# One layer's feed forward started by token tile: residual's bias added ahead, output units parked, first products halved

## The chip, the cores and the metric

The kernel runs on 1 core of one Trainium2 chip. Its time is the device time of one launch in microseconds (us). The engines are TensorE (PE; its weight loads are listed apart as PEld), VectorE (DVE), ScalarE (ACT), GpSimd (POOL) and SyncE (SP), whose queue issues most DMAs. Each engine works through its own list of instructions in order.

## The reference, cut to what matters

A trunk of two layers over 256 latent tokens and 256 context tokens of width 1024, in float32. Layer 1 (the second) has no context output, so its feed forward runs over the 256 latent tokens alone: two token tiles of 128.

```
m  = gated_merge of four token mixers            # out = m @ w_out + b_out
x  = layer_norm(ALPHA * x + g1 * out, ln1_g, ln1_b)
h  = layer_norm(x) * (1 + sc2) + sh2             # features of the feed forward
u  = dwconv(h @ w1 + b1)                         # 2 x 2816 columns, 3 taps over tokens
f  = (silu(gate) * val) @ w2 + b2
x  = layer_norm(ALPHA * x + g2 * f, ln2_g, ln2_b)
```

c, the conditioning vector, gives sh1 to g2 through `w_ada`: six blocks of 1024 columns per layer.

## The kernel before

Every product is taken in three parts for precision: both operands are split into a high part in float32r and a low remainder, and `mm3` (L225 to L227) issues high x high, low x high and high x low, each a 128x128 weight load and a matmul. Weights come as 1 MB blocks `raw` (two buffers, SyncE's queue, L163); `split` (L196/L194 and L198) makes `wh` on ScalarE or POOL and `wl` on VectorE or POOL, in a ring of four `wh` and four `wl`. Who casts follows a table `POOL[layer][phase]`: with (a, b, c, d), POOL takes the high part of every unit whose number leaves b when divided by a, and the remainder of every unit that leaves d when divided by c.

The layers run one after the other. In a layer, `mixer` runs four branches: recurrent, differential attention, grouped attention (`gqa`), neighbourhood attention (`na`, whose first steps are the products of n_q and n_k, evicted as `nx` at L1112). `merge` multiplies each with its branch weight and a gate into `macc`. `out_stage` then does the out projection (`acc`, eight units of w_out rows; `order` says which unit meets which token tile when) and the epilogue by token tile: `epilogue` (gate times sum, residual, layer norm with its gain and bias), `normalise` (the next layer norm, `xn`), and, once both tiles are through, `to_fm`, which transposes `xn` (`tps`, L328), applies scale and shift (`h`, L337 on VectorE and L340 on ScalarE) and splits into `hh` (POOL, L342) and `hl` (VectorE, L344).

`epilogue_prep` runs at the head of `out_stage`. It loads the gate row g and the bias row bo (L1192), doubles bo on ScalarE (L1205), multiplies both to gb on POOL (L1210), and adds gb to the residual x (L1213), the first 512 columns on VectorE, the other 512 on POOL.

Of w_out's eight units four are kept outside the ring (`wo`, made in `merge` of branch 3), the other four go through the ring. Then come the units of the feed forward: `ffn` takes them in eleven pairs, a pair being 512 columns of w1 (four units of 128 output columns, `us[0] + us[1]`), each unit 8 x 3 products over 256 tokens, evicted by ScalarE (`up`, `cv`), and the convolution's outer taps on VectorE (L1269).

`ada_step` is one quarter of a block of the w_ada product: a 1 MB load, 8 matmuls of 256 columns in column groups of 32 (16 records), and one addition (L365) on VectorE; `pump` runs steps at given places. Ahead of layer 1's first pair `pump(4)` runs the last ones, of which three have work: they belong to g2 of layer 1.

What is computed, and in which order each engine does it, is set by the order of the calls and by a scheduling layer that lays the engines' lists out. Names: `acc` is a PSUM sum of the out projection, `x_4402` and `x_4404` the two token tiles of the residual, `nmu`, `rs`, `rt`, `rstd`, `sqb`, `sqh`, `rh`, `lnb` are 128x1 statistics.

Of the kernel before, what the change touches and what calls it, by code (L numbers as in the profile page):

```python
# [8 lines left out]
F32 = mybir.dt.float32  # L9
F32R = mybir.dt.float32r  # L10
# [8 lines left out]
T = 512  # L19
# [82 lines left out]

POOL = (((4, 0, 8, 2), (4, 0, 8, 2), (4, 0, 8, 0), (5, 2, 8, 2), (6, 5, 8, 2)), ((4, 0, 4, 1), (4, 0, 4, 2), (4, 0, 100, 6), (4, 0, 4, 2), (2, 0, 4, 0)))


LATE = ((8, 8, 4, 8), (8, 8, 4, 8))
# [2 lines left out]
class Trunk:  # L111
# [32 lines left out]
    def features(self, name, w):  # L144

        out = []
        for part in "hl":
            ts = [self.Q(name + part) for _ in range(w // 128)]
            vs = [view(t, 1024 // w, w) for t in ts]
            out.append([vs[2 * j * w // 1024][:, 2 * j % (1024 // w):2 * j % (1024 // w) + 2, :] for j in range(4)])  # L150
        return out

    def S(self, name, n=1, bufs=3):
        return self.sm.tile([128, n], F32, tag=f"{name}", name=name, bufs=bufs)
# [71 lines left out]
        nc.tensor.matmul(out, lhsT=lh, rhs=rl, start=False, stop=False)  # L226
        return nc.tensor.matmul(out, lhsT=ll, rhs=rh, start=False, stop=stop)  # L227

    def fm_split(self, units, h):

        tags = [("mm", 3)] * 3 + [("o", 1)]
        ps = [self.ps.tile([128, 512], F32, tag=tags[n][0], name="mm", bufs=tags[n][1]) for n in range(len(units))]
        for a, b in ((0, SEG), (SEG, T)):
            for (hi, lo), p in zip(units, ps):
                for k in range(KD):
                    self.mm3(p[:, a:b], hi[:, k, :], lo[:, k, :], h[0][k // 2][:, k % 2, a:b],
                             h[1][k // 2][:, k % 2, a:b], k == 0, k == KD - 1)
        return ps

    def fm(self, unit, h, slices, hold=None):  # L240
        hi, lo = unit
# [325 lines left out]
    def mixer(self, l, x, hT, pool, tags):  # L567
        nc, i = self.nc, self.i
        self.pool, self.tags = pool, tags
        self.l = l  # L570
        self.with_ctx = l < DEPTH - 1
        self.hT = hT
        w = i["w_in"][l]
        self.w = w
        self.full = [(0, T)] if l == 0 else [(0, 256), (256, 512)]
        self.all = [(0, T)]
        self.lat = [(256, 512)]
        self.own = self.all if self.with_ctx else self.lat
        self.tsl = slice(0, T) if self.with_ctx else slice(SEG, T)
        self.macc = None  # L580
        if l == 1:
            us = [u for col in ("a_x", "d_k") for u in self.cols_fm(w, COL[col])]
            self.pump(PUMP[2], "s")
            ps = self.fm_split(us, hT)
            self.pre_fm = {COL["a_x"]: ps[0:2], COL["d_k"]: ps[2:4]}
        self.events, self.ready, self.phase = [], None, 0
        y = self.lru()
        gates = self.gates(0)
        self.events, self.ready, self.phase = [], None, 1
        diff = self.diff()  # L590
        next(diff)
        self.merge(0, y, gates)
        self.after_branch(1, next(diff))
        self.events, self.ready, self.phase = [], None, 2
        y = self.gqa()
        self.after_branch(2, y)
        self.events, self.ready, self.phase = [], None, 3
        y = self.na()
        self.after_branch(3, y)
# [32 lines left out]
    def merge(self, j, y, gates):  # L632
# [4 lines left out]
        if j == 3:  # L637
            box = [view(self.B("wo"), 4, D) for _ in range(2)]
            store = [None] * 2 + [lambda n=n: [(box[0][:, n, :], box[1][:, n, :])] for n in range(4)] + [None] * 2
            self.out_units = self.out_rows(self.i["w_out"][self.l], store)  # L640
            self.out_units(2), self.out_units(4)
        self.rate = rate if j < 3 else 0.0
# [554 lines left out]
    def epilogue_prep(self, l, x, segs, alloc, dep, blk, bname):  # L1197

        nc, i = self.nc, self.i
        g = {s: self.bcast(alloc, self.g_dram[l, blk][(0 if s == LAT else 1):(1 if s == LAT else 2), :], dep)  # L1200
             for s in segs}
        b = self.bcast(lambda: self.E("bo")[:, 0:512], i[bname][l:l + 1, :], dep)
        if blk == 2:
            for n in range(2):
# [2 lines left out]
        for s in segs:  # L1207
            for n in range(2):
                gb = self.E("gb")[:, 0:512]
                nc.gpsimd.tensor_tensor(out=gb, in0=g[s][n], in1=b[n], op=ALU.mult)  # L1210
                for t in x[s]:
                    xs = t[:, 512 * n:512 * n + 512]
                    eng[n].tensor_tensor(out=xs, in0=xs, in1=gb, op=ALU.add)  # L1213
        return g

    def epilogue(self, x, us, acc, g, lng, lnb, lnb_mean):

# [23 lines left out]
    def ffn(self, l, hT, nseg, apool):  # L1241
# [2 lines left out]
        W = SEG * nseg  # L1244
        w1 = i["ffn_w1"][l]
        self.a = []
        self.phase = 4
        for pair in range(NFF // 2):
            us = [list(self.cols_fm(w1, off + 256 * pair)) for off in (0, DFF)]
            if pair == 0:  # L1250
                self.pump(PUMP[0] if l == 0 else 4, "s")
            pre = self.fm_split(us[0] + us[1], hT) if pair == 0 and nseg == 2 else None
            for ci in range(2):
                jj = 2 * pair + ci
                conv = []
# [24 lines left out]
    def run(self):  # L1280
# [105 lines left out]
        self.W = SEG  # L1386
        with tc.tile_pool(name="mix1", bufs=1, reuse_waits="tile") as mp:
            self.l, self.pool = 1, mp
            self.mixer(1, None, hT, mp, {"gate": 16})
            alloc = lambda: mp.tile([128, 512], F32, tag="macc", name="epi", bufs=8)  # L1390
            x, hT2 = self.out_stage(1, {LAT: x[LAT]}, alloc, self.last_gate, (LAT,), self.m, self.out_units, KD, 8, range(2, 6), 2,
                                    "b_out", "ln1", (1, 3))
# [21 lines left out]
    def out_stage(self, l, x, alloc, dep, segs, src, units, nk, resident, kept, blk, bname, lnn, nxt):  # L1414
# [23 lines left out]
        order += [(t, k, both) for t in range(max(nt - 2, 1), nt - 1) for k in kept]  # L1438
        order += [(nt - 1, k, (n,)) for n in both for k in kept]
        self.project((srch, srcl), units, nk, order, acc)  # L1440
        hT = self.features("h", SEG * len(segs)) if nxt else None
        for s in segs:
            xn = []
            for t in range(2):
# [3 lines left out]
                if nxt:  # L1448
                    self.normalise(x[s][t], hv, nmu)
                    xn.append(hv)  # L1450
            if nxt:
                for _ in self.to_fm(*nxt, s, xn, hT[0], hT[1], SEG * segs.index(s),
                                    tags=(("t", 2), ("mm", 3) if nt == 2 else ("t", 2) if s == LAT else ("s", 2))):
                    pass
# [41 lines left out]
```

## Time and profile before

| what | value |
|---|---|
| median of 3 runs (lowest to highest) | 1539.54 us (1537.94 to 1542.12) |
| the profiled execution | 1543.09 us, of it span 1541.3 us |
| TensorE busy | 1429.6 us, 93% of the span |
| VectorE, ScalarE, POOL busy | 977.6, 638.8, 506.1 us |
| weight products `mm` (L225 to L227) of 256 and 512 columns, three parts | 507.2 + 502.2 + 502.9 us of latency, 1488 each |
| HBM read | 208.23 MB, 136 GB/s over the span |

A timeline's row gives the start in us from the span's start, the length in us, engine, line, operation, output<-input, its size and how many instructions of one kind the row holds; in square brackets stands the time for which the engine was idle before, and what released it. Lengths of matmuls overlap: the pace is read from the starts. In a row of windows, the granted clock of TensorE is a share of 2.4 GHz, 0.50 being 1.2 GHz.

### The profile page before, as it was taken

Reading aid. Unit: us, or ns where it says so; the run is one execution under the profiler, and the core shown is the slowest. Engines: PE = TensorE matmul, PEld = TensorE weight load, DVE = VectorE, ACT = ScalarE, POOL = GpSimd, SP = SyncE. Lnnn points to the kernel's source line nnn. Section 1 sums busy time; section 2 is a strip of 40 time slices with the busy share of each in tenths; the row PEclk is TensorE's granted clock in tenths of the full one; section 3 lists DMA queues with packets and bytes.
Section 4 is the critical chain, followed back from the end, with each engine's and each line's share of the span. In section 5 each row is a group of like instructions: output and inputs, shape, how many; then the busy total and the mean of one; then the engine's idle time right before and its main releaser. Section 6 shows DMA issues by size and latency. Waiting matters only on the chain.

```text
span 1541.3 us, 22344 instructions
## 1 busy us (share of the span) xinstructions
PE 1429.6 (93%) x8420; PEld 1176.3 (76%) x8420; DVE 977.6 (63%) x1691; ACT 638.8 (41%) x1136; POOL 506.1 (33%) x614
## 2 busy tenths in 40 slices
PE   5989998989999999999999999988998997899997
PEld 3757776967887777777778887887787986799876
DVE  4664655753533997554555437776875648799965
ACT  3452253233244345444444223471625353555532
POOL 2241001431432613221222412241132545366662
PEclk9999999989999999999999999998899999799999
DMA  9335612302623545444453432434432436454463
GB/s 345 118 116 184 190 69 72 127 29 67 207 81 111 179 139 167 163 138 164 160 169 124 149 133 74 145 109 141 157 129 84 146 126 208 138 165 164 165 218 109
DMA packets 149022, 218.90 MB, mean 142 GB/s; under 512 B 9990, under 2 KB 118882, under 8 KB 148914
## 3 DMA queue, kind: packets, MB, share of 16 engines
q1 hardware_dynamic: 146402, 212.74, 41.5%
q0 software_dynamic: 2512, 4.73, 1.1%
q8 instruction: 67, 1.10, 0.3%
q14 instruction: 41, 0.34, 0.1%
HBM read 208.23 MB, written 1.08 MB: 136 GB/s over the span
## 4 chain that ended last, share of the span: by engine, by line
PE 53%; DVE 12%; issue 5%; ACT 4%; DMA 4%; POOL 2%; DVEq 0%; SPq 0%; ACTq 0%; POOLq 0%
PE mm L225 12%; PE mm L226 12%; PE mm L227 11%; PE acc L227 3%; PE acc L226 3%; PE acc L225 3%; DVE wl L198 3%; DVE cv L1269 3%; PE ops L867 2%; PE adaps L362 2%; ACT wh L196 2%; PE tp L859 1%; DMA raw<-in_w_out_dram 1%; DMA raw<-in_ffn_w_dram 1%; POOL cv L1273 1%
## 5 line engine op out<-in xcount | busy, mean ns | idle before, releaser
L225 PE MATMUL mm<-hh,wh 128*128 128x256 f32 (+1 forms) x1488 | 507.2, 344 | 17.0 <-ACT gate L626 4.5
L227 PE MATMUL mm<-hh,wl 128*128 128x256 f32 (+1 forms) x1488 | 502.9, 339 | 4.5 <-DVE wl L198 3.2
L226 PE MATMUL mm<-hl,wh 128*128 128x256 f32 (+1 forms) x1488 | 502.2, 338 | 0.4 <-DVE hl L344 0.3
L198 DVE TENSOR_TENSOR wl<-raw,wh 128x1024 fp32r<-128x1024 f32 x211 | 285.8, 1362 | 176.5 <-ACT wh L196 136.8
L225 PEld LDWEIGHTS mm<-hh,wh 128*128 128x128 f32 x1488 | 287.3, 194 | 63.0 <-issue 17.2
L227 PEld LDWEIGHTS mm<-hh,wl 128*128 128x128 f32 x1488 | 287.5, 193 | 38.7 <-DVE wl L198 5.0
L196 ACT CAST wh<-raw 128x1024 fp32r<-128x1024 f32 x181 | 188.5, 1047 | 309.3 <-PE mm L226 128.1
L226 PEld LDWEIGHTS mm<-hl,wh 128*128 128x128 f32 x1488 | 287.9, 194 | 32.4 <-issue 3.6
L1269 DVE SCALAR_TENSOR_TENSOR cv<-up,par,cv 128x512 f32<-128x512 f32 (+1 forms) x176 | 156.5, 898 | 45.5 <-ACT cv L1266 33.2
L194 POOL TENSOR_SCALAR wh<-raw 128x1024 fp32r<-128x1024 f32 x74 | 89.6, 1211 | 282.9 <-PE acc L227 51.6
L198 POOL TENSOR_TENSOR wl<-raw,wh 128x1024 fp32r<-128x1024 f32 x44 | 119.0, 2704 | 129.5 <-ACT wh L196 112.0
L1273 POOL TENSOR_TENSOR cv<-cv 128x512 f32<-128x512 f32 (+1 forms) x44 | 53.5, 1216 | 158.7 <-ACT cv L1272 158.7
L226 PE MATMUL acc<-wl,a 128*128 128x512 f32 x232 | 92.3, 398 | 3.8 <-DVE wl L198 2.9
L227 PE MATMUL acc<-wh,a 128*128 128x512 f32 x232 | 92.1, 398 | 0.0
L225 PE MATMUL acc<-wh,a 128*128 128x512 f32 x232 | 91.0, 397 | 0.0
L843 DVE TENSOR_REDUCE nm<-sps 128x1 f32<-128x512 f32 (+1 forms) x96 | 56.3, 598 | 53.0 <-PE sps L888 36.9
L844 ACT ACTIVATE e<-sps,nm 128x512 f32<-128x512 f32 (+1 forms) x96 | 59.0, 617 | 64.1 <-DVE nm L843 50.3
L225 PE MATMUL mm<-wh,hh 128*128 128x256 f32 x240 | 68.6, 286 | 0.0
L227 PE MATMUL mm<-wh,hl 128*128 128x256 f32 x240 | 68.3, 284 | 0.0
L226 PE MATMUL mm<-wl,hh 128*128 128x256 f32 x240 | 67.7, 282 | 0.0
L293 ACT ACTIVATE junk<-x,nmu 128x512 bf16<-128x512 f32 x44 | 31.7, 721 | 85.0 <-DVE nmu L285 47.3
L1272 ACT ACTIVATE cv<-cv 128x512 f32<-128x512 f32 (+1 forms) x44 | 23.1, 525 | 91.4 <-DVE cv L1269 91.4
(312 smaller groups left out, 2324.5 us busy)
## 6 DMA issues: line engine op xcount, KB each, us to landing
raw<-in_ffn_w_dram SPq DMA_DIRECT2D x66, 1024.0 KB
raw<-in_w_in_dram SPq DMA_DIRECT2D x52, 1024.0 KB
raw<-in_w_ada_dram SPq DMA_DIRECT2D x40, 1024.0 KB
raw<-in_w_branch_dram SPq DMA_DIRECT2D x8, 1024.0 KB
raw<-in_w_out_dram SPq DMA_DIRECT2D x8, 1024.0 KB
w<-in_w_ada_dram SPq DMA_DIRECT2D x4, 1024.0 KB
w<-in_w_ada_dram SPq DMA_DIRECT2D x8, 512.0 KB
qk<-dp SPq DMA_DIRECT2D x48, 64.0 KB
```

The source lines that it names most:

```text
L194: nc.gpsimd.tensor_scalar(out=hi, in0=src, scalar1=1.0, scalar2=0.0, op0=ALU.mult, op1=ALU.add)
L196: nc.scalar.copy(hi, src)
L198: eng.tensor_tensor(out=lo, in0=src, in1=hi.bitcast(F32), op=ALU.subtract)
L225: nc.tensor.matmul(out, lhsT=lh, rhs=rh, start=start, stop=False)
L226: nc.tensor.matmul(out, lhsT=lh, rhs=rl, start=False, stop=False)
L227: return nc.tensor.matmul(out, lhsT=ll, rhs=rh, start=False, stop=stop)
L293: nc.scalar.activation(self.junk, halves[n], AF.Square, bias=nmu, accum_out=q[n])
L362: nc.tensor.matmul(ps[32 * g:32 * g + 32, :], lhsT=self.silu_c[:, kk + k2, :], rhs=raw[:, k2, 256 * g:256 * g + 256], start=(k2 == 0), sto ...
L843: nc.vector.tensor_reduce(out=nm, in_=s if fold is None else fold, op=ALU.max, axis=AX.X, negate=True)
L844: nc.scalar.activation(e, s, AF.Exp, bias=nm, accum_out=total)
L1269: nc.vector.scalar_tensor_tensor(out=cv, in0=up[:, :, k:k + 256], scalar=tap[k], in1=cv, op0=ALU.mult, op1=ALU.add)
L1273: nc.gpsimd.tensor_tensor(out=conv[0], in0=conv[0], in1=conv[1], op=ALU.mult)
```

## The change

Four things, all in layer 1:

1. `residual()` is taken out of `epilogue_prep`. For layer 1's mixer it runs earlier, in `mixer` between the grouped attention's merge and the neighbourhood attention: the loads of g and bo, bo x 2, gb, and x + gb.
2. Units 6 and 7 of w_out no longer go through the ring: their parts are stored in tiles of other pools (`pt_tile`, `X`).
3. `tile_to_fm` makes the features of the feed forward as soon as one token tile is normalised: eight transposes, scale and shift in steps of 128 tokens in turn on VectorE and ScalarE, the cast on POOL, the remainder on VectorE. The first pair's products are cut in two: all four units over the first 128 tokens, then over the other 128, so that 96 products of 256 columns become 192 of 128.
4. The three ada steps stand between these products instead of ahead of them, and a new entry (2, 0, 100, 99) of the table holds for the first pair: POOL casts every second high part, and VectorE all remainders.

```diff
@@ -104,3 +104,3 @@
 
-POOL = (((4, 0, 8, 2), (4, 0, 8, 2), (4, 0, 8, 0), (5, 2, 8, 2), (6, 5, 8, 2)), ((4, 0, 4, 1), (4, 0, 4, 2), (4, 0, 100, 6), (4, 0, 4, 2), (2, 0, 4, 0)))
+POOL = (((4, 0, 8, 2), (4, 0, 8, 2), (4, 0, 8, 0), (5, 2, 8, 2), (6, 5, 8, 2)), ((4, 0, 4, 1), (4, 0, 4, 2), (4, 0, 100, 6), (4, 0, 4, 2), (2, 0, 4, 0), (2, 0, 100, 99)))
 
@@ -152,2 +152,24 @@
 
+    def tile_to_fm(self, l, blk, t, xn, boxes, tag):
+
+        nc = self.nc
+        mod = self.modT[l]
+        ts = slice(128 * t, 128 * t + 128)
+        for n in range(2):
+            ps = view(self.ps.tile([128, 512], F32, tag=tag[0], name="tps", bufs=tag[1]), 4, 128)
+            for k in range(4):
+                nc.tensor.transpose(ps[:, k, :], xn[n][:, 128 * k:128 * k + 128], self.ident)
+            h32 = view(self.E("h32"), 4, 128)
+            for k in range(4):
+                sc = mod[:, (blk + 1) * 8 + 4 * n + k, 0:1]
+                sh = mod[:, blk * 8 + 4 * n + k, 0:1]
+                if k % 2 == 0:
+                    nc.vector.tensor_scalar(out=h32[:, k, :], in0=ps[:, k, :], scalar1=sc, scalar2=sh, op0=ALU.mult,
+                                            op1=ALU.add)
+                else:
+                    nc.scalar.activation(h32[:, k, :], ps[:, k, :], AF.Identity, bias=sh, scale=sc)
+            hi, lo = boxes[0][n][:, :, ts], boxes[1][n][:, :, ts]
+            nc.gpsimd.tensor_scalar(out=hi, in0=h32, scalar1=1.0, scalar2=0.0, op0=ALU.mult, op1=ALU.add)
+            nc.vector.tensor_tensor(out=lo, in0=h32, in1=hi.bitcast(F32), op=ALU.subtract)
+
     def S(self, name, n=1, bufs=3):
@@ -228,7 +250,8 @@
 
-    def fm_split(self, units, h):
+    def fm_split(self, units, h, cuts=((0, SEG), (SEG, T)), tags=(("mm", 3), ("mm", 3), ("mm", 3), ("o", 1))):
 
-        tags = [("mm", 3)] * 3 + [("o", 1)]
         ps = [self.ps.tile([128, 512], F32, tag=tags[n][0], name="mm", bufs=tags[n][1]) for n in range(len(units))]
-        for a, b in ((0, SEG), (SEG, T)):
+        for n, (a, b) in enumerate(cuts):
+            if n:
+                yield ps
             for (hi, lo), p in zip(units, ps):
@@ -237,3 +260,3 @@
                              h[1][k // 2][:, k % 2, a:b], k == 0, k == KD - 1)
-        return ps
+        yield ps
 
@@ -596,2 +619,5 @@
         self.after_branch(2, y)
+        if l == 1:
+            g = self.bcast(lambda: self.E("gr")[:, 0:512], self.g_dram[1, 2][0:1, :], None)
+            self.residual(1, x, (LAT,), {LAT: g}, None, 2, "b_out")
         self.events, self.ready, self.phase = [], None, 3
@@ -639,2 +665,4 @@
             store = [None] * 2 + [lambda n=n: [(box[0][:, n, :], box[1][:, n, :])] for n in range(4)] + [None] * 2
+            if self.l:
+                store[6:8] = [lambda: [[self.pt_tile("wo") for _ in range(2)]], lambda: [[self.X("wo", F32R) for _ in range(2)]]]
             self.out_units = self.out_rows(self.i["w_out"][self.l], store)
@@ -1201,2 +1229,9 @@
              for s in segs}
+        if (l, blk) != (1, 2):
+            self.residual(l, x, segs, g, dep, blk, bname)
+        return g
+
+    def residual(self, l, x, segs, g, dep, blk, bname):
+
+        nc, i = self.nc, self.i
         b = self.bcast(lambda: self.E("bo")[:, 0:512], i[bname][l:l + 1, :], dep)
@@ -1213,3 +1248,2 @@
                     eng[n].tensor_tensor(out=xs, in0=xs, in1=gb, op=ALU.add)
-        return g
 
@@ -1246,8 +1280,17 @@
         self.a = []
-        self.phase = 4
+        self.phase = 4 if nseg == 2 else 5
         for pair in range(NFF // 2):
             us = [list(self.cols_fm(w1, off + 256 * pair)) for off in (0, DFF)]
+            pre = None
             if pair == 0:
-                self.pump(PUMP[0] if l == 0 else 4, "s")
-            pre = self.fm_split(us[0] + us[1], hT) if pair == 0 and nseg == 2 else None
+                if nseg == 2:
+                    self.pump(PUMP[0], "s")
+                    pre = list(self.fm_split(us[0] + us[1], hT))[-1]
+                else:
+
+                    part = self.fm_split(us[0] + us[1], hT, ((0, 128), (128, SEG)), [("mm", 3)] * 3 + [("s", 2)])
+                    next(part)
+                    self.pump(4, "s")
+                    pre = next(part)
+                    self.phase = 4
             for ci in range(2):
@@ -1388,3 +1431,3 @@
             self.l, self.pool = 1, mp
-            self.mixer(1, None, hT, mp, {"gate": 16})
+            self.mixer(1, x, hT, mp, {"gate": 16})
             alloc = lambda: mp.tile([128, 512], F32, tag="macc", name="epi", bufs=8)
@@ -1440,3 +1483,8 @@
         self.project((srch, srcl), units, nk, order, acc)
-        hT = self.features("h", SEG * len(segs)) if nxt else None
+        one = nxt and len(segs) == 1
+        if one:
+            boxes = [[view(self.Q("h" + p), 4, SEG) for _ in range(2)] for p in "hl"]
+            hT = [[bs[j // 2][:, 2 * (j % 2):2 * (j % 2) + 2, :] for j in range(4)] for bs in boxes]
+        else:
+            hT = self.features("h", SEG * len(segs)) if nxt else None
         for s in segs:
@@ -1450,3 +1498,5 @@
                     xn.append(hv)
-            if nxt:
+                    if one:
+                        self.tile_to_fm(*nxt, t, hv, boxes, ("t", 2))
+            if nxt and not one:
                 for _ in self.to_fm(*nxt, s, xn, hT[0], hT[1], SEG * segs.index(s),
```

VectorE's list where the epilogue of the out projection begins. Before (`wl` are remainders of the feed forward's first units):

```order
L803 TENSOR_TENSOR ml<-macc,mh 128x256 x2
L198 TENSOR_TENSOR wl<-raw,wh 128x1024
L1213 TENSOR_TENSOR x_4402<-x_4402,gb 128x512
L1213 TENSOR_TENSOR x_4404<-x_4404,gb 128x512
L1427 TENSOR_SCALAR lnm<-lm_11758,lm_11759 128x1
L1223 TENSOR_TENSOR acc<-acc,epi 128x512 x2
L1225 SCALAR_TENSOR_TENSOR x_4402,s_11893<-acc,x_4402 128x512
L1225 SCALAR_TENSOR_TENSOR x_4402,s_11892<-acc,x_4402 128x512
L198 TENSOR_TENSOR wl<-raw,wh 128x1024
L285 TENSOR_SCALAR nmu<-s_11892,s_11893 128x1
L1229 SCALAR_TENSOR_TENSOR xn,s_11895<-x_4402,nmu,epi 128x512
L1229 SCALAR_TENSOR_TENSOR xn,s_11894<-x_4402,nmu,epi 128x512
L198 TENSOR_TENSOR wl<-raw,wh 128x1024
```

And with the change:

```order
L220 TENSOR_TENSOR wl<-raw,wh 128x1024 x2
L831 TENSOR_TENSOR ml<-macc,mh 128x256 x2
L220 TENSOR_TENSOR wl<-raw,wh 128x1024 x2
L1470 TENSOR_SCALAR lnm<-lm_11762,lm_11763 128x1
L1257 TENSOR_TENSOR acc<-acc,epi 128x512 x2
L1259 SCALAR_TENSOR_TENSOR x_4402,s_11897<-acc,x_4402 128x512
L1259 SCALAR_TENSOR_TENSOR x_4402,s_11896<-acc,x_4402 128x512
L308 TENSOR_SCALAR nmu<-s_11896,s_11897 128x1
L1263 SCALAR_TENSOR_TENSOR xn,s_11899<-x_4402,nmu,epi 128x512
L1263 SCALAR_TENSOR_TENSOR xn,s_11898<-x_4402,nmu,epi 128x512
L318 TENSOR_SCALAR sqb<-sq_11909 128x1
L319 TENSOR_SCALAR sqh<-sq_11909 128x1
```

The two x additions have left the list here, and both remainders that stood inside the epilogue are now ahead of `lnm`.

TensorE's list behind the last product of the out projection. Before:

```order
L226 MATMUL acc<-wo,mh 128x512
L227 MATMUL acc<-wo,ml 128x512
L362 MATMUL adaps<-raw,silu_c 32x256 x24
L328 MATMUL tps<-cst,xn 128x128 x16
L225 MATMUL mm<-hh,wh 128x256 x3
L226 MATMUL mm<-hl,wh 128x256
L227 MATMUL mm<-hh,wl 128x256
```

And with the change:

```order
L248 MATMUL acc<-wo,mh 128x512
L249 MATMUL acc<-wo,ml 128x512
L161 MATMUL tps<-cst,xn 128x128 x8
L247 MATMUL mm<-hh,wh 128x128 x4
L385 MATMUL adaps<-raw,silu_c 32x256 x8
L248 MATMUL mm<-hl,wh 128x128
L249 MATMUL mm<-hh,wl 128x128
```

The 24 ada matmuls stood ahead of 16 transposes of both tiles; now eight transposes of tile 0 come first, then four products of 128 columns, then eight ada matmuls.

VectorE's list at the start of branch 3 (`mt` closes the grouped attention's merge). Before:

```order
L662 SCALAR_TENSOR_TENSOR mt<-gate,mm 128x256 x6
L198 TENSOR_TENSOR wl<-raw,wh 128x1024 x2
L1112 TENSOR_SCALAR nx<-mm,par 128x256
L803 TENSOR_TENSOR qk<-nx,qk 64x256 x2
L1112 TENSOR_SCALAR nx<-mm,par 128x256
L198 TENSOR_TENSOR wl<-raw,wh 128x1024
L803 TENSOR_TENSOR qk<-nx,qk 64x256 x2
L1112 TENSOR_SCALAR nx<-mm,par 128x512
```

And with the change:

```order
L690 SCALAR_TENSOR_TENSOR mt<-gate,mm 128x256 x6
L220 TENSOR_TENSOR wl<-raw,wh 128x1024 x3
L1248 TENSOR_TENSOR x_4402<-x_4402,gb 128x512
L1248 TENSOR_TENSOR x_4404<-x_4404,gb 128x512
L1140 TENSOR_SCALAR nx<-mm,par 128x256 x2
L831 TENSOR_TENSOR qk<-nx,qk 64x256 x3
L1140 TENSOR_SCALAR nx<-mm,par 128x512
```

A third `wl` and the two additions to x stand ahead of the first `nx`.

## Rows read from the trace of the kernel before

**Rows 1.** Windows by engine: us, busy us (instructions), granted clock PEclk, DMA share, GB/s.

```profile
1305.00:1310.00 5.00, 1.94 (x16) 0.68 (x16) 4.63 (x16) 1.22 (x4) 0.00 (x0) 0.56 0.97 377
1340.00:1360.00 20.00, 20.00 (x169) 20.00 (x169) 18.96 (x22) 10.79 (x23) 13.14 (x22) 1.00 0.50 161
```

**Rows 2.** Timeline of PE: start us, us, engine, line, output<-input, tile, [idle before <-releaser].

```profile
1301.16 0.39 PE L227 MATMUL acc<-wo,ml 128*128 128x512 f32 x1
1307.92 1.94 PE L362 MATMUL adaps<-raw,silu_c 128*32 128x256 f32 x16 [6.37 <-DMA raw<-in_w_ada_dram]
1317.13 1.97 PE L328 MATMUL tps<-cst,xn 128*128 128x128 f32 x8
1323.92 1.30 PE L225 MATMUL mm<-hh,wh 128*128 128x256 f32 x3 [1.73 <-POOL hh L342]
1329.49 0.29 PE L225 MATMUL mm<-hh,wh 128*128 128x256 f32 x1
```

**Rows 3.** Timeline of VectorE (DVE), layer 1's first epilogue.

```profile
1293.43 3.47 DVE L1213 TENSOR_TENSOR x<-x,gb 128x512 f32<-128x512 f32 x2 [2.74 <-POOL gb L1210]
1296.94 1.28 DVE L1223 TENSOR_TENSOR acc<-acc,epi 128x512 f32<-128x512 f32 x2
1299.35 3.30 DVE L198 TENSOR_TENSOR wl<-raw,wh 128x1024 fp32r<-128x1024 f32 x1
1308.74 0.27 DVE L1237 TENSOR_SCALAR nmu<-nmu,rstd,lnm 128x1 f32<-128x1 f32 x1
1315.35 0.54 DVE L315 TENSOR_SCALAR xn<-x,rstd,lnb 128x512 f32<-128x512 f32 x1
1322.02 1.90 DVE L337 TENSOR_SCALAR h<-tps,modT 128x256 f32<-128x256 f32 x4 [0.98 <-PE tps L328]
```

**Rows 4.** Timeline of SyncE's queue (SPq): DMA issues around the out projection.

```profile
1280.31 1.20 SPq L1192 DMA_DIRECT2D epi<-g  x2
1284.77 0.92 SPq L1192 DMA_DIRECT2D bo<-in_b_out_dram  x2
1288.11 0.38 SPq L163 DMA_DIRECT2D raw<-in_ffn_w_dram  x1
1312.70 0.37 SPq L163 DMA_DIRECT2D raw<-in_ffn_w_dram  x1
```

**Rows 5.** Timeline of ScalarE (ACT) and GpSimd (POOL), the same stretch.

```profile
1309.04 0.72 ACT L293 ACTIVATE junk<-x,nmu 128x512 bf16<-128x512 f32 x1 [3.08 <-DVE nmu L1237]
1292.08 2.56 POOL L1210 TENSOR_TENSOR gb<-epi,bo 128x512 f32<-128x512 f32 x2 [3.14 <-ACT bo L1205]
1323.25 3.24 POOL L342 TENSOR_SCALAR hh<-h 128x512 fp32r<-128x512 f32 x4 [1.30 <-ACT h L340]
```

**Rows 6.** Timeline of TensorE's weight loads (PEld), at the full and the half clock.

```profile
1112.98 0.53 PEld L975 LDWEIGHTS nb<-cst,os 128*128 128x128 f32 x4
1113.43 0.19 PEld L227 LDWEIGHTS mm<-hh,wl 128*128 128x128 f32 x1
1175.33 0.19 PEld L225 LDWEIGHTS mm<-hh,wh 128*128 128x128 f32 x1
1175.44 0.19 PEld L226 LDWEIGHTS mm<-hl,wh 128*128 128x128 f32 x1
1325.05 0.29 PEld L226 LDWEIGHTS mm<-hl,wh 128*128 128x128 f32 x1
1325.21 0.34 PEld L227 LDWEIGHTS mm<-hh,wl 128*128 128x128 f32 x1
```

**Rows 7.** Timeline of PE, an ada step at the full clock.

```profile
1050.36 1.07 PE L362 MATMUL adaps<-raw,silu_c 128*32 128x256 f32 x16
```

**Rows 8.** Timelines of VectorE and GpSimd at the start of branch 3.

```profile
1205.49 0.47 DVE L1112 TENSOR_SCALAR nx<-mm,par 128x256 f32<-128x256 f32 x1
1212.03 0.75 DVE L1112 TENSOR_SCALAR nx<-mm,par 128x512 f32<-128x512 f32 x1 [1.04 <-PE mm L227]
1204.44 3.38 POOL L198 TENSOR_TENSOR wl<-raw,wh 128x1024 fp32r<-128x1024 f32 x1
```

More of the change, by code (lines that the diff above doesn't have):

```diff
@@ L583, in mixer @@
             self.pump(PUMP[2], "s")
-            ps = self.fm_split(us, hT)
+            ps = list(self.fm_split(us, hT))[-1]
             self.pre_fm = {COL["a_x"]: ps[0:2], COL["d_k"]: ps[2:4]}
```

## The prediction

> **What bounds the kernel now.** I read the stretch from the last product of layer 1's out projection to the second pair of its feed forward, because the change lies there but for one small move. The windows come first [rows 1]: from 1340 us on TensorE is busy 20.00 of 20 us at the full clock and VectorE 18.96, so what the first pair loses or gains is carried on by TensorE to the end. Between 1305 and 1310 TensorE has 1.94 us of work in 5, and its granted clock is 0.56. TensorE's timeline shows the hole [rows 2]: the last acc product starts at 1301.16, the first feed forward product at 1323.92; between them lie three ada steps of 16 records (1.94 us for the first) and 16 transposes. VectorE's timeline says why [rows 3]: it starts on the sums only at 1296.94, since 3.47 us of residual additions stand ahead; a weight remainder of 3.30 us and others stand inside the epilogue; nmu2 of token tile 0 is out at 1308.74, its normalised half at 1315.35, and no transpose goes before that.
>
> **The start of the first pair.** I replay the new order with the old durations. Without four entries of SP's queue (the two of bo take 0.92 us, the two of the gate alike) the last weight load of the first pair is issued about 2 us earlier than 1288.11 [rows 4] and lands as much earlier; the remainders of the four units then end on VectorE at 1294.9, and the sums start there instead of at 1296.94. The 3.47 us of additions are gone from this place, so are the remainders within the epilogue: nmu2 of tile 0 comes at 1303.5, 5.2 us earlier. The normalised tile needs two passes on ScalarE (0.72 us each, [rows 5]) and, since tile 1's statistics are queued ahead of it on VectorE, two more: 1308.15 instead of 1315.35. Eight transposes take 1.97 us at the half clock [rows 2], the features three small steps in turn on VectorE and ScalarE (1.90 us for 4 steps of 256 columns, [rows 3]; 128 columns lie between half of that and all) with two steps of tile 1 between them, and the POOL cast 0.81 us (3.24 for 4, [rows 5]). The first product can start at 1313.5, 10.4 us earlier than 1323.92. Bounds: a microsecond either way.
>
> **What the halved products cost.** 96 products of 256 columns become 192 of 128, each with its own 128x128 weight load. Before, the pair runs from 1323.92; the clock rises at about 1329.49 [rows 2], where 24 are done; the other 72 go at 0.118 us (169 in 20 us, [rows 1]) to 1338.1. No product of this kind with 128 columns is in the trace, so I bound it. Below: half of 0.118, 0.06 us, if the streaming sets it. Above: 0.225 us, the plain f32 products of 128 columns, which take two records each, four in 0.45 us (1112.98 to 1113.43, [rows 6]). I take the spacing of two weight loads where no product holds the second back: 1175.33 to 1175.44, 0.11 us [rows 6], in this same kind of product. At the half clock the same place shows 1325.05 to 1325.21, 0.165 us. So halving the columns saves next to nothing: 192 x 0.11 = 21 us stand against 96 x 0.118 = 11.3.
>
> Here a rule speaks for the change. The Trainium skill, "TensorE: Matmul & The Clock Gate", section "Back-to-back issue gap", states about 81 ns for a sustained pair of load and product at 128 columns; by it 192 would take 15.6 us, and the sum below would come out near -1.5 us. No row here shows a load of this kind that follows within 81 ns, and the 0.11 us of [rows 6] speak against it.
>
> **The ada steps.** Three of four remaining pumps have work. Before, all three lie in the hole and cost nothing. Now one stands behind the fourth product, one behind tile 0, one behind the first unit of tile 1, all on TensorE's path: 1.94 us at the half clock [rows 2], 1.0 each at the full one (1.07 with its tail, [rows 7]).
>
> **The sum at the end of the pair.** From 1313.5: 23 products at 0.165 (3.8), the first ada step (1.9), then, with a rise 5.6 us after the first product as at 1323.92 to 1329.49, 169 products at 0.111 (18.8), tile 1's eight transposes (0.9, half of their 1.97 at the half clock) and two ada steps (2.0): 27.4 us, 1340.9. Before: 1338.1. That is **+2.8 us**. Tile 1's vector work is hidden beside tile 0's products; VectorE's first tap of the convolution follows unit 0, which ends some 2.5 us later than now, so VectorE loses the same and neither makes it good.
>
> **The start of branch 3.** The residual's additions move there. VectorE issues the branch's first nx at 1205.49 and the third at 1212.03 [rows 8]. Now two additions stand ahead of it, and wait for POOL, whose gb follows a remainder from 1204.44 for 3.38 us [rows 8] and takes 2.56 for two [rows 5]: nx comes at about 1211.3 to 1213.3. Its PSUM bank is one of three, the fourth group starts near 1212. TensorE stalls for 0 to 1.8 us; I take 0.9. What the additions and gb cost besides, the POOL and DMA gaps there hide; if they didn't, up to 3.4 us.
>
> **Parked units.** Units 6 and 7 off the ring free the slots for the pair's weights. This is what lets VectorE's remainders end at 1294.9; the out projection's own end, 1301.4, stays, since its products run without a gap [rows 2]. No other gain.
>
> The total is 2.8 + 0.9 = +3.7 us: the profiled execution, 1543.09 us with a span of 1541.3, would become 1546.8; against the median of 1539.54 (the profiled one lies 3.55 above it) I forecast **1543.3 us**. A measurement here tells 0.3%, 4.6 us, from no change.
>
> **Rivals.**
> 1. *The clock doesn't rise in the pair.* A product of 128 columns in 0.165 us streams less than one of 256 in 0.21, which is what raised the clock before. From 1305 to 1310 TensorE worked 1.94 us of 5 and was granted 0.56 [rows 1]; the clock rose in the dense stretch from 1323.92 [rows 2]. No row shows a long stretch of loads with half-length products. If the rise waits for the transposes of tile 1, about ten products more run at 0.165 and those transposes at half speed: +1.8 on the forecast. If it waits for a later ada step, +5 to +10. If it never comes, 192 x 0.165 = 31.7, three steps at 1.94 and 1.97 of transposes, 39.5 us from 1313.5: the pair ends at 1353, +16 in all (1555). It decides by the clock in the windows 1315 to 1340.
> 2. *Products of 128 columns fall to the f32 price.* 192 x 0.225 = 43.2 + 5.0 us: the pair ends at 1361.7, +24.5 in all (1564). Against it: these products take one record each at 256 columns.
> 3. *The load hides behind the streaming* (not slower). At 0.06 us, 169 products take 10.1 instead of 18.8 and the 23 early ones 2.5 instead of 3.8: the pair ends at 1330.9, -6.3 in all. But its weights then come late: the loads for the second pair wait for ada steps 2 and 3, as now from 1312.70 on [rows 4], go out near 1325, and need some 7 us to land and be split, which gives back about 2: -4.3 (1535). It decides below 0.09 us a product, where the time comes out even; at 0.08 it gives -1.5 (1538). The rule of the Trainium skill named above ("TensorE: Matmul & The Clock Gate") would be this case.
> 4. *The second pair's weights are late in the forecast itself.* Steps 2 and 3 end near 1329.3 and 1333; loads then issued land some 5 us later and are split by 1337.5 and 1342, for units needed at 1340.9 and 1343.8. The margin is under 3 us; a few per cent of contention would add 1 to 3 us (1545).
>
> **How the numbers follow.** Forecast with its rise of the clock, give or take 3 us: 0.50. Rival 1 with a rise at the transposes or later 0.17, never 0.06. Rival 2: 0.10. Rival 3, or an earlier start than replayed: 0.12. Rival 4: 0.05. The forecast's 0.50 splits at +4.6 into 0.31 same and 0.19 slower; rival 1 gives 0.04 same and 0.19 slower, rivals 2 and 4 0.02 same and 0.13 slower, rival 3 0.07 same (between 0.07 and 0.09 us a product it is lost in the noise) and 0.05 faster. With 0.08 moved to faster for a start that the replay has too late by more than a microsecond or a stall that isn't there, 0.05 of it from same and 0.03 from slower: 0.13 faster, 0.39 same, 0.48 slower. The range leaves out rival 2, part of rival 1's worst case and the best end of rival 3: 1535 to 1556. The likeliest case alone is 1540 to 1546.5.
>
> **What would show it.** Right: the first feed forward product near 1313.5 plus what branch 3 adds, 128-column products 0.11 us apart at the full clock, ada steps between them, the first pair's end some 3 us later than before, and an unchanged pace behind it. Wrong: products under 0.09 or over 0.15 us apart at the full clock; a granted clock of 0.5 up to 1340 or beyond; TensorE idle for weights ahead of the second pair; a gap of over 2 us at branch 3's fourth group; or a first product later than 1316.

## The result and the profile after

The changed kernel took 1559.58 us (median of 4 runs, 1548.82 to 1566.65) against 1540.83 us before (4 runs): a ratio of 1.012 with a 95% interval of 1.0076 to 1.0164. It is 18.75 us slower, where the forecast was 1543.3, some 3.7 us slower, with a range of 1535 to 1556. The profiled execution took 1566.65 us, span 1564.9 us, against 1543.09 and 1541.3 before; it is the longest of the four, so what its trace shows is more than the loss of the median.

The windows of the changed kernel: behind the stretch and its length come the busy times of TensorE, its weight loads, VectorE, ScalarE and POOL; the granted clock is the third number from the end.

```profile
1305.00:1310.00 5.00, 1.57 (x8) 1.17 (x6) 4.14 (x12) 1.72 (x4) 0.74 (x1) 0.50 0.00 0
1315.00:1320.00 5.00, 5.00 (x25) 5.00 (x25) 0.45 (x1) 0.71 (x1) 0.00 (x0) 0.50 0.47 186
1325.00:1330.00 5.00, 5.00 (x26) 5.00 (x25) 0.00 (x1) 0.00 (x0) 0.00 (x0) 0.50 0.01 3
1345.00:1350.00 5.00, 5.00 (x25) 5.00 (x25) 1.01 (x2) 1.04 (x1) 1.21 (x2) 0.50 0.61 206
1360.00:1380.00 20.00, 20.00 (x153) 20.00 (x153) 16.38 (x20) 9.61 (x21) 9.37 (x18) 0.90 0.47 152
```

From 1315 on TensorE is busy 5.00 of 5 us, and its clock stays at 0.50, 1.2 GHz, to the end of the first pair at 1359. Before, it rose 5.6 us into the pair [rows 2] and stood at 1.00 behind that, in the pair and later [rows 1]:

```profile
1330.00:1335.00 5.00, 5.00 (x44) 5.00 (x43) 2.48 (x4) 2.48 (x5) 1.19 (x5) 1.00 0.00 0
```

TensorE's timeline in the changed kernel, the lines that answer to [rows 2]:

```profile
1304.60 1.97 PE L161 MATMUL tps<-cst,xn 128*128 128x128 f32 x8 [5.45 <-ACT xn L337]
1310.20 1.12 PE L247 MATMUL mm<-hh,wh 128*128 128x128 f32 x4 [3.62 <-POOL hh L172]
1311.24 1.94 PE L385 MATMUL adaps<-raw,silu_c 128*32 128x256 f32 x16
1319.36 1.93 PE L161 MATMUL tps<-cst,xn 128*128 128x128 f32 x8
1334.55 1.94 PE L385 MATMUL adaps<-raw,silu_c 128*32 128x256 f32 x16
1341.73 1.94 PE L385 MATMUL adaps<-raw,silu_c 128*32 128x256 f32 x16
1359.02 0.52 PE L247 MATMUL mm<-hh,wh 128*128 128x256 f32 x1
1364.20 0.28 PE L247 MATMUL mm<-hh,wh 128*128 128x256 f32 x1
```

The pair did start early: 1310.20 is 11.4 us behind the last acc product (1298.77 in this execution), where it had been 22.8 (1301.16 to 1323.92, [rows 2]). But the second pair starts only at 1359.02: the pair took 48.8 us, not 14.2. The clock rises only among the second pair's whole products, at about 1364.1. From the last acc product to the second pair it is 60.3 us instead of 36.9, which is +23.3; some 2.3 come on top for the second pair's first products at 1.2 GHz, and 2.4 go off because this execution reached the last acc product earlier. That makes +23.2 of the +23.6 of the spans. The 2.4 are no gain of the change: TensorE's last wait for `mt` ahead of branch 3 ended at 1190.96 instead of 1195.85, 4.9 us earlier and ahead of anything that was moved, and 2.5 of that was lost again up to the last acc product. In e5_cut (below), whose code is that of the kernel before up to the pair, the same wait ended at 1190.87.

The pace of the halved products, TensorE's timeline and that of its weight loads:

```profile
1313.60 0.41 PE L247 MATMUL mm<-hh,wh 128*128 128x128 f32 x1
1313.81 0.41 PE L248 MATMUL mm<-hl,wh 128*128 128x128 f32 x1
1314.03 0.41 PE L249 MATMUL mm<-hh,wl 128*128 128x128 f32 x1
```

```profile
1313.49 0.33 PEld L247 LDWEIGHTS mm<-hh,wh 128*128 128x128 f32 x1
1313.70 0.33 PEld L248 LDWEIGHTS mm<-hl,wh 128*128 128x128 f32 x1
1313.92 0.33 PEld L249 LDWEIGHTS mm<-hh,wl 128*128 128x128 f32 x1
```

By their starts, load and product take turns: load 1313.49, product 1313.60, load 1313.70, product 1313.81. A halved product costs 0.213 us here (69 of them from 1344.30 to 1359.02 take 14.72 us). That is what a whole one cost at this clock before:

```profile
1326.93 0.41 PE L225 MATMUL mm<-hh,wh 128*128 128x256 f32 x1
1327.14 0.41 PE L226 MATMUL mm<-hl,wh 128*128 128x256 f32 x1
1327.36 0.41 PE L227 MATMUL mm<-hh,wl 128*128 128x256 f32 x1
```

The columns are halved, the time of a product isn't, and there are twice as many.

At branch 3 the wait that was forecast is there, in the list of TensorE's waits between 1195 and 1225 (us in total, times, longest), in VectorE's timeline and in the windows:

```profile
PE mm L247 <- DVE nx L1140: 2.1, 1, 2.1
```

```profile
1205.20 3.45 DVE L1248 TENSOR_TENSOR x<-x,gb 128x512 f32<-128x512 f32 x2
1208.57 0.86 DVE L1140 TENSOR_SCALAR nx<-mm,par 128x256 f32<-128x256 f32 x2
```

```profile
1205.00:1210.00 5.00, 2.91 (x25) 2.73 (x24) 4.92 (x6) 0.87 (x3) 4.92 (x4) 1.00 0.63 217
1210.00:1215.00 5.00, 5.00 (x32) 5.00 (x31) 4.84 (x8) 1.98 (x4) 2.47 (x4) 0.66 0.48 114
```

These windows hold 25 and 32 products; before there were 44 in each:

```profile
1205.00:1210.00 5.00, 5.00 (x44) 5.00 (x43) 4.47 (x6) 2.67 (x5) 2.83 (x1) 1.00 0.66 219
1210.00:1215.00 5.00, 5.00 (x44) 5.00 (x43) 3.62 (x7) 1.24 (x2) 2.12 (x3) 1.00 0.61 148
```

Behind the wait of 2.1 us the granted clock is 0.66 for a window. 31 products of 0.12 us make 3.7 us; by the last acc product 2.5 us of them are left.

### The profile page after: what moved, and what is told of

It reads as the page before. It is cut to its first block, busy times and chain, and to the rows that moved or that the text cites. A ratio compares the mean times of both kernels' runs of the same rounds, so it can differ in the third digit from the quotient of the medians.

```text
span 1564.9 us, 22542 instructions
## 1 busy us (share of the span) xinstructions
PE 1455.0 (93%) x8516; PEld 1203.1 (77%) x8516; DVE 975.7 (62%) x1696; ACT 640.2 (41%) x1140; POOL 501.1 (32%) x613
## 4 chain that ended last, share of the span: by engine, by line
PE 55%; DVE 10%; DMA 4%; issue 4%; ACT 4%; POOL 3%; DVEq 0%; SPq 0%; ACTq 0%; POOLq 0%
PE mm L247 13%; PE mm L248 12%; PE mm L249 12%; PE acc L248 3%; PE acc L249 3%; PE acc L247 3%; DVE wl L220 3%; PE adaps L385 2%; PE ops L895 2%; DMA raw<-in_ffn_w_dram 1%; PE tp L887 1%; DVE cv L1312 1%; ACT wh L218 1%; DMA raw<-in_w_in_dram 1%; POOL macc L693 1%
## 5 line engine op out<-in xcount | busy, mean ns | idle before, releaser
L247 PE MATMUL mm<-hh,wh 128*128 128x256 f32 (+2 forms) x1520 | 522.7, 347 | 20.9 <-ACT gate L652 6.0
L249 PE MATMUL mm<-hh,wl 128*128 128x256 f32 (+2 forms) x1520 | 518.5, 342 | 4.9 <-DVE wl L220 3.3
L248 PE MATMUL mm<-hl,wh 128*128 128x256 f32 (+2 forms) x1520 | 518.1, 342 | 0.2 <-DVE hl L367 0.2
L220 DVE TENSOR_TENSOR wl<-raw,wh 128x1024 fp32r<-128x1024 f32 x210 | 277.2, 1328 | 187.3 <-ACT wh L218 148.7
L247 PEld LDWEIGHTS mm<-hh,wh 128*128 128x128 f32 x1520 | 301.6, 200 | 67.5 <-issue 21.8
L249 PEld LDWEIGHTS mm<-hh,wl 128*128 128x128 f32 x1520 | 301.8, 199 | 38.5 <-DVE wl L220 5.1
L248 PEld LDWEIGHTS mm<-hl,wh 128*128 128x128 f32 x1520 | 302.5, 199 | 32.0 <-issue 3.6
L220 POOL TENSOR_TENSOR wl<-raw,wh 128x1024 fp32r<-128x1024 f32 x43 | 113.9, 2650 | 129.0 <-ACT wh L218 119.7
L316 ACT ACTIVATE junk<-x,nmu 128x512 bf16<-128x512 f32 x44 | 31.7, 721 | 84.4 <-DVE nmu L308 45.8
L1305 ACT ACTIVATE up<-mm,par 128x512 f32<-128x512 f32 (+1 forms) x88 | 51.0, 579 | 30.8 <-PE mm L249 25.7
```

What stands on the lines that cost most here:

```text
L220: eng.tensor_tensor(out=lo, in0=src, in1=hi.bitcast(F32), op=ALU.subtract)
L247: nc.tensor.matmul(out, lhsT=lh, rhs=rh, start=start, stop=False)
L316: nc.scalar.activation(self.junk, halves[n], AF.Square, bias=nmu, accum_out=q[n])
L1305: nc.scalar.activation(up[:, :, 1:257], view(ps, 2, 256)[:, 0:nseg, :], AF.Identity, bias=par[:, R_B1 + j:R_B1 + j + 1])
```

## The experiments

Theory A: halved products that start at 1.2 GHz don't bring the clock up, and a pair at that pace is the loss. Theory B: a halved product is slow at any clock. Theory C: the loss comes from the residual's new place. Ratios are to runs of the kernel before that were taken beside them on the same chip; in brackets stands the 95% interval.

**e1_wide: the changed kernel with the pair's products whole again**, and with the ada steps ahead of them, as before.

```diff
-                    part = self.fm_split(us[0] + us[1], hT, ((0, 128), (128, SEG)), [("mm", 3)] * 3 + [("s", 2)])
-                    next(part)
                     self.pump(4, "s")
-                    pre = next(part)
```

> The changed kernel, but the first pair's products stay whole (96 of 256 columns) and the three ada steps stand ahead of them, as before; residual ahead, parked units and features by tile stay. Theory A (halved products hold the clock at 1.2 GHz for the whole pair, 0.213 us each, and that is where the time goes): the clock rises within 6 us of the pair's first product, the pair takes 14 us, and the time is 1537 to 1542. Theory B (a halved product is slow at any clock): the same here. Theory C (the loss comes from the moved residual and branch 3): the time stays over 1550.

1543.44 us, ratio 1.0023 (1.0004 to 1.0043), 1.4 us above the expected 1537 to 1542. All but 3 us of the loss is gone with the halves and the ada steps between them: theory C falls. What is left of the change gains nothing: its pair starts 22.9 us behind the last acc product (1301.90 to 1324.80), as before, since whole products wait for tile 1.

**e2_warm: fillers keep the clock up** (34 products of 512 columns whose sums nothing reads).

```diff
+    def fill(self, count, after):
+        ps = self.ps.tile([128, 512], F32, tag="mm", name="fill", bufs=3)
+        with self.tc.issue_after(after.ins):
+            for _ in range(count):
+                self.nc.tensor.matmul(ps, lhsT=self.m[0][0][:, 0, 0:128], rhs=self.out_units(5)[0][0], start=True, stop=True)
...
+            self.fill(20, self.last_acc)
...
+        if t == 0:
+            self.fill(14, tps)
```

> The changed kernel with 20 filler products of 512 columns behind the out projection and 14 behind tile 0's transposes; nothing reads them. They keep the array streaming up to the pair's first product. Theory A: the granted clock is 1.00 at the first product and stays there, the 192 products go 0.11 us apart, the pair ends 17 us earlier than in the changed kernel, 1543 to 1548. Theory B: the clock is 1.00 but the products stay 0.2 us apart, 1558 to 1566. Theory C: over 1550 with products 0.11 apart.

1543.59 us, ratio 1.002 (1.0004 to 1.0036). Its timeline, loads and windows:

```profile
1309.89 3.51 PE L1213 MATMUL fill<-wo,mh 128*128 128x512 f32 x14
1313.76 0.66 PE L249 MATMUL mm<-hh,wh 128*128 128x128 f32 x4 [0.36 <-POOL hh L172]
1339.54 0.34 PE L249 MATMUL mm<-hh,wh 128*128 128x256 f32 x1
```

```profile
1319.14 0.19 PEld L249 LDWEIGHTS mm<-hh,wh 128*128 128x128 f32 x1
1319.25 0.19 PEld L250 LDWEIGHTS mm<-hl,wh 128*128 128x128 f32 x1
1319.37 0.19 PEld L251 LDWEIGHTS mm<-hh,wl 128*128 128x128 f32 x1
```

```profile
1320.00:1325.00 5.00, 5.00 (x48) 5.00 (x47) 2.29 (x5) 1.79 (x4) 1.27 (x4) 1.00 0.00 2
1335.00:1340.00 5.00, 5.00 (x47) 5.00 (x46) 3.26 (x4) 3.18 (x6) 2.10 (x7) 1.00 0.64 217
```

The same 192 products go 0.11 us apart and the clock stays 1.00: theory B falls, theory A stands. The pair takes 25.8 us, and the second one starts 36.8 us behind the last acc product (1302.73), against 36.9 before. So even with the clock up, the early start buys nothing: the pair starts 11.7 us earlier and takes 11.6 us longer, with the doubled loads and the ada steps in it.

**e5_cut: the kernel before, with nothing but the pair's products halved** (all four units over tile 0, then over tile 1). Left out here are the lines of `fm_split` that take the cuts and give the fourth unit another PSUM tag.

```diff
-            pre = self.fm_split(us[0] + us[1], hT) if pair == 0 and nseg == 2 else None
+            pre = self.fm_split(us[0] + us[1], hT, *(() if nseg == 2 else (((0, 128), (128, SEG)),))) if pair == 0 else None
```

> The kernel before with only the first pair's products cut in two (all four units over tile 0, then over tile 1; 192 products of 128 columns); features of both tiles, ada steps and residual as before. Theory A (halved products started at 1.2 GHz keep it there): the pair runs 0.213 us a product to its end, 41 us instead of 14, no tile 1 transposes or ada steps lie between them that could raise the clock: 1565 to 1570. Theory B (it is the order of the other work, the halves only cost the 0.11 us load): the clock rises within 6 us as before, 1549 to 1552.

1565.59 us, ratio 1.0174 (1.0147 to 1.0201). The pair ran from 1319.91 to 1361.21, 41.3 us, and one of its windows reads

```profile
1345.00:1350.00 5.00, 5.00 (x25) 5.00 (x25) 2.10 (x3) 0.93 (x2) 1.12 (x3) 0.50 0.00 0
```

That is 25 products where the kernel before had 44 a window. The cut alone costs 25 us, with the residual, the parked units, the features and the ada steps left as they were.

**e13_kick: 14 fillers behind tile 0's transposes only**, when the clock has fallen already.

Against e2_warm:

```diff
-        if nxt and len(segs) == 1:
-            self.fill(20, self.last_acc)
```

> The changed kernel with the 14 fillers behind tile 0's transposes alone, none behind the out projection: the clock has fallen by then. Theory A: the fillers raise the clock themselves, and halved products that follow at once keep it: granted clock 1.00 for most of the pair, products 0.11 us apart, 1544 to 1552 (the fillers take up to 2 to 3 us at the lower clock). If halved products let the clock fall whatever stood ahead: 1560 to 1570.

1545.85 us, ratio 1.0027 (1.0008 to 1.0047).

```profile
1310.00:1315.00 5.00, 4.86 (x16) 4.19 (x17) 3.81 (x12) 1.93 (x6) 0.20 (x1) 0.50 0.00 0
1320.00:1325.00 5.00, 5.00 (x48) 5.00 (x46) 2.11 (x7) 1.72 (x3) 0.00 (x0) 1.00 0.55 202
```

The fillers start at the lower clock and raise it, and the halved products that follow at once run at 1.00 to the end of the pair: here they do not push it down. Theory A's expected 1544 to 1552 holds.

**e4_nores: the changed kernel with the residual back at the out projection.**

```diff
-            self.residual(1, x, (LAT,), {LAT: g}, None, 2, "b_out")
...
-        if (l, blk) != (1, 2):
-            self.residual(l, x, segs, g, dep, blk, bname)
+        self.residual(l, x, segs, g, dep, blk, bname)
```

> The changed kernel with the residual back at the out projection. Theories A and B: no wait at branch 3, the pair starts some 3 us later, and the halved products still run 0.213 us apart at 1.2 GHz for most of the pair: 1548 to 1566, with a spread like the changed kernel's. Theory C: 1536 to 1543.

1568.52 us, ratio 1.0189 (1.0174 to 1.0204): the clock stood at 0.50 from 1302.5 to 1367.3. Theory C falls a second time. The time lies above the expected 1548 to 1566, and the expected spread did not come: the four runs lie between 1567.9 and 1570.4.

**e3_res, e7_late and e9_latepark: the other parts, on the kernel before.** e3_res moves the residual alone, to the change's place; e7_late puts it behind the neighbourhood attention; e9_latepark is e7_late with units 6 and 7 parked as well. First e3_res, then what e9_latepark adds:

```diff
         y = self.na()
+        if l == 1:
+            g = self.bcast(lambda: self.E("gr")[:, 0:512], self.g_dram[1, 2][0:1, :], None)
+            self.residual(1, x, (LAT,), {LAT: g}, None, 2, "b_out")
         self.after_branch(3, y)
```

```diff
+                store[6:8] = [lambda: [[self.pt_tile("wo") for _ in range(2)]], lambda: [[self.X("wo", F32R) for _ in range(2)]]]
```

> The kernel before with the residual moved ahead of branch 3 and nothing else. Theories A and B: TensorE waits 2 us at branch 3 for nx (and may lose a further 2 us to a lower clock there), and the epilogue begins 2 to 4 us earlier: 1538 to 1544. Theory C: 1548 or more.

> The kernel before with the residual moved, as in e3_res, but behind the neighbourhood attention instead of ahead of it. If the 2.1 us wait for nx and the clock it costs are what the early place loses: no wait there, the epilogue's gain of 3 us stays, 1536 to 1539. If the epilogue's gain is not there: 1540 to 1542.

> e7_late with units 6 and 7 parked as in the change. If parking brings the epilogue forward by taking the weight remainders out of it: 2 us faster than e7_late. If not: the same as e7_late.

e3_res: 1542.35 us, 1.0017 (0.9998 to 1.0036). Its epilogue is faster, first feed forward product 19.7 us behind the last acc instead of 22.8, but its TensorE waits 2.1 us for nx at branch 3. e7_late: 1540.12, 0.9995 (0.9979 to 1.0010). It has no wait for nx and the epilogue's gain is there (19.4 us), yet its time lies in the range that was expected without that gain, and its interval overlaps that of e3_res. e9_latepark: 1536.79, **0.9981 (0.9966 to 0.9996)**, 0.2% faster than the kernel before. Its first product comes 14.4 us behind the last acc (1297.63):

```profile
1306.43 1.86 PE L328 MATMUL tps<-cst,xn 128*128 128x128 f32 x8
1309.22 1.10 PE L328 MATMUL tps<-cst,xn 128*128 128x128 f32 x8 [0.94 <-DVE xn L315]
1312.04 1.24 PE L225 MATMUL mm<-hh,wh 128*128 128x256 f32 x3 [1.72 <-POOL hh L342]
```

So two of the change's parts together, in a later place, gain a little; what parking adds to e7_late is not shown by the times, whose intervals overlap. Whole products start at +14.4 here.

**e8_best, e12_warmlate, e11_fill9: attempts at more.** e8_best: ada steps and 22 fillers ahead of the pair, late residual, three of four units halved. e12_warmlate: e2_warm with the late residual. e11_fill9: e9_latepark with 17 fillers ahead of the third ada step and 3 ahead of the last transposes. The core of the edits of e8_best, then of e11_fill9:

```diff
-                    part = self.fm_split(us[0] + us[1], hT, ((0, 128), (128, SEG)), [("mm", 3)] * 3 + [("s", 2)])
-                    next(part)
-                    self.pump(4, "s")
-                    pre = next(part)
+                    pre = list(self.fm_split((us[0] + us[1])[0:3], hT, ((0, 128), (128, SEG)), [("mm", 3)] * 3))[-1]
...
+            with self.tc.issue_after(self.last_acc.ins):
+                self.pump(2, "s")
+            self.fill(14, self.last_adamm)
```

```diff
+                self.fill(3, self.last_tps)
...
+            self.pump(2, "s")
+            self.fill(17, self.last_adamm)
+            with self.tc.issue_after(self.last_fill.ins):
+                self.pump(2, "s")
```

> The changed kernel with the residual behind the neighbourhood attention, the three ada steps in the hole ahead of the first product, 22 filler products that keep the clock up, and only three of the four units halved. Theory A: the clock stays 1.00, 144 halved products at 0.112 us and 24 whole ones at 0.119 follow a start 11 us behind the last acc product, the pair ends 30 to 31 us behind it instead of 36.7: 1533 to 1537. If the fillers delay the transposes, or the second pair's weights come late: 1538 to 1543.

> e2_warm (the changed kernel with 34 fillers) with the residual behind the neighbourhood attention, so that the wait for nx at branch 3 is gone too. Theory A: e2_warm's time less the 2 to 4 us of branch 3: 1539 to 1542, no gain over the kernel before, since the halved products and the ada steps in the pair eat the early start. If the early start were worth more than that: 1536 or less.

> e9_latepark (residual late, units parked, whole products, features of both tiles at once) with 17 fillers ahead of the third ada step and 3 ahead of the last transposes. If the lower clock in the hole still costs there: the clock stays 1.00 up to the pair and the time is 2 to 3 us under e9_latepark, 1533 to 1535. If the fillers only take the place of idle time: within 1 us of it, 1536 to 1538.

e8_best missed: 1553.20 us, 1.0096 (1.0073 to 1.0119), where 1533 to 1543 was expected. The clock was 1.00 at its first halved product; then it read

```profile
1310.21 0.55 PE L252 MATMUL mm<-hh,wh 128*128 128x128 f32 x3 [0.90 <-POOL hh L172]
1311.96 0.33 PE L253 MATMUL mm<-hl,wh 128*128 128x128 f32 x1 [1.21 <-DVE hl L173]
```

```profile
1310.00:1315.00 5.00, 3.59 (x22) 3.45 (x23) 3.33 (x11) 1.93 (x5) 2.52 (x6) 0.81 0.37 129
1315.00:1320.00 5.00, 5.00 (x26) 5.00 (x25) 1.03 (x4) 0.81 (x1) 0.00 (x0) 0.50 0.00 0
```

Behind these two short waits the halved products fell to 0.21 us apart, from 1313.3 on. The clock came back once, among the halved products behind tile 1's transposes, and left again, behind two waits of 0.50 and 0.58 us:

```profile
1325.00:1330.00 5.00, 3.91 (x26) 3.63 (x25) 3.13 (x6) 1.72 (x4) 1.20 (x2) 0.82 0.00 0
1330.00:1335.00 5.00, 5.00 (x27) 5.00 (x26) 0.00 (x0) 0.00 (x0) 0.00 (x0) 0.52 0.00 0
```

That the waits made it fall is argued from this one trace, not shown by an experiment.

e12_warmlate: 1543.88, 1.0025 (1.0010 to 1.0040), no gain over e2_warm and above the expected 1539 to 1542. The list of its TensorE's waits from 1200 on has no wait for nx any more, but these two in its place:

```profile
PE mm L249 <- ACT gate L654: 1.4, 1, 1.4
PE mm L250 <- DVE yl L948: 1.1, 1, 1.1
```

All traces with the late residual show both, ahead of the out projection (e7_late, e9_latepark, e8_best, e11_fill9 too), and no other trace does. So the later place saves the wait for nx and brings waits of 2.5 us, which fits that neither e7_late nor e12_warmlate gained by it.

e11_fill9: 1537.12, 0.9980 (0.9969 to 0.9992), the same as e9_latepark, and inside the 1536 to 1538 expected if the fillers only take idle time. But they did not hold the clock up to the pair: it was 0.78 from 1310 to 1315 and 0.50 from 1315 to 1320, ahead of the first product at 1318.86. What a clock held there would be worth with whole products is not shown.

## Why the prediction was wrong

- **The step that failed** is in the sum at the end of the pair: "with a rise 5.6 us after the first product as at 1323.92 to 1329.49". It took the rise of whole products for halved ones. The clock never rose in the profiled pair. From that, 169 products cost 0.213 instead of 0.111 us (+17.2), two ada steps and the transposes twice their price (+2.9). e5_cut shows the same with the cut alone, and e13_kick shows it gone once fillers have raised the clock.
- **The second size** is the halved product at 1.2 GHz: 0.165 us was forecast from 1325.05 to 1325.21 [rows 6], but that pair of loads stood at the head of a stretch, behind a wait. In a steady run it is 0.213; twice its own 0.11 us of the full clock, 0.22, would have been nearer. The 23 early products cost +1.1, and with the terms above the 27.4 us of the sum become 48.6, against 48.8 measured. It also made rival 1 too cheap: 1555 for "never", where 192 x 0.213 gives 41 us instead of 31.7, some 1564; so the range ended at 1556. The mechanism of rival 1 is what happened; it got 0.23 of the chance in all, 0.06 for "never".
- **At the full clock** the terms held: 0.11 us a product in e2_warm as taken from 1175.33 to 1175.44 [rows 6], and the pair took 25.8 us where 27.4 were summed with some of it at 1.2 GHz. That e2_warm's 1543.59 is near the forecast 1543.3 is luck: the forecast loses 2.8 us in the pair, and e2_warm, with its fillers and its earlier start, loses nothing from the last acc product to the second pair (36.8 against 36.9). Rival 3 and the 81 ns of the Trainium skill ("TensorE: Matmul & The Clock Gate", section "Back-to-back issue gap") fall: 0.11 us is the pace of these products at the full clock in e2_warm. The prediction's estimate from that page, -1.5 us, is its total with branch 3; the sum at the end of the pair alone would be -2.3. Rival 2 falls with them: its pair of 48.2 us is close to the measured 48.8 by luck, since the slow pace goes with the clock of 1.2 GHz and is gone at 2.4.
- **The start** was right: forecast 10.4 us earlier, measured 11.4 (22.8 to 11.4 behind the last acc product).
- **Branch 3** was undersized: 0.9 us forecast, 0 to 1.8 the range, where a wait of 2.1 and the fallen clock cost 3.7, of which 2.5 were left at the last acc product. e3_res, with the epilogue's gain in it, is 2 us slower, which is not clear of noise (0.9998 to 1.0036).
- Rival 4, late weights, did not show: TensorE had no wait between the first pair and the second, whose weights had the long pair to arrive in.
- The spread of the changed kernel (1548.8 to 1566.7) fits a clock that rises part way in some runs: the mean granted clock was 0.955 and 0.958 in the two long runs, 0.967 and 0.972 in the two short ones. e8_best's trace shows that a rise part way can happen, behind tile 1's transposes; of the changed kernel only a long run has a trace, so this part is argued, not shown.

## What to carry to other kernels

When products are cut to fewer columns, price them together with their weight loads, and at both clocks: here 128 columns took 0.112 and 0.213 us, where 256 took 0.119 and 0.213. Ask what will bring the clock back up behind an idle stretch, and look for a row in which just that kind of work did it: here whole products and 512-column fillers did, and halved ones did not, although the profile shows TensorE busy throughout. An early start for one engine is worth its distance only after the extra work that buys it is taken off; here some 11.7 us of start paid for 11.6 us of loads and steps, before any clock.

## What the runs showed of the hardware that was not expected

- A TensorE that the profile shows busy 5.00 of 5 us kept a granted clock of 0.50 for 44 us (1315 to 1359 in the changed kernel). The Trainium skill, "TensorE: Matmul & The Clock Gate", section "What's actually happening", has activity release the clock and names a busy engine as the state of 2.4 GHz; these runs show busy time, as the profile counts it, without that.
- The same 192 products ran their whole length at 1.00 where the clock stood there at their start (e2_warm, e13_kick), and at 0.50 where it stood there (the changed kernel, e4_nores, e5_cut). In e8_best, with 144 of them, it went from 1.00 to 0.50 behind waits of 0.90 and 1.21 us, and came back for 3.5 us. What in the halved products keeps the clock from rising stays open.
- At 1.2 GHz the starts of a weight load and of a product of 128 columns took turns, some 0.107 us apart; at 2.4 GHz load and product together took 0.112 us (e2_warm).
